# First mixer: decays by exp and tanh, its products on VectorE, the logarithm's series behind the pools

## The chip, the cores and the metric

The kernel runs on one core of a Trainium2 chip, as one launch. The metric is its time on the device in microseconds; below it is the median of three runs. A profile is one further execution, recorded by the hardware. The engines are named as in the profile: PE is TensorE's products, PEld its weight loads, DVE is VectorE, ACT is ScalarE, POOL is GpSimd, SP is the engine whose queue issues nearly all DMAs.

## The reference, cut to what matters

The program is a two-layer block, then a block with a recurrent part, a neighbourhood attention and 32 experts. The change lies in the first layer's mixer and in the keys of the cross attention behind it:

```python
def rg_lru(x, w_gx, b_gx, w_ga, b_ga, lam):
    xh = x.reshape(Bn, S, H_A, HD_A)
    gate_x = jax.nn.sigmoid(jnp.einsum('bshi,hij->bshj', xh, w_gx).reshape(Bn, S, W) + b_gx)
    gate_a = jax.nn.sigmoid(jnp.einsum('bshi,hij->bshj', xh, w_ga).reshape(Bn, S, W) + b_ga)
    log_a = -C_RG * gate_a * jax.nn.softplus(-lam)      # C_RG = 8
    a = jnp.exp(log_a)
    mult = jnp.sqrt(-jnp.expm1(2.0 * log_a))
    bx = mult * (gate_x * x)
    h = scan over time: h = a * h + bx
    return h

def mixer_ab(x, ...):                                   # x is 512 x 1024, float32
    z = rms_norm(x, norm) @ w_in                        # 1024 x (1024 gate, 1024 rec, 512 pool)
    xr = causal_dwconv(z_rec, conv_w, conv_b)           # 4 taps
    y_a = jax.nn.gelu(z_gate) * rg_lru(xr, w_gx, b_gx, w_ga, b_ga, lam)
    y_b = multi_scale_pool(z_pool, w_pool, b_pool, pool_scale)   # windows 2, 4, 8, 16
    return jnp.concatenate([y_a, y_b], axis=-1) @ w_out

def cross_attn(x, mem, ...):
    m = rms_norm(mem, mem_norm)                         # mem is 256 x 1024
    k = m @ wk;  v = m @ wv
```

The softplus of lam is a logarithm, which the kernel computes on 8 numbers per partition by a series.

## The kernel before, in words

Activations lie with the features on the 128 partitions and the 512 tokens along the row, so the eight tiles of a 1024 wide vector are called 0 to 7. Every product is made of three single ones (`mm3`, lines 522 to 524): weight and activation are each split into a rounded high part and the rest (whi and wlo, xn or act or tmp likewise), and high by high, high by low and low by high are added in PSUM.

Weights come as a stream of 1 MB chunks in the order of use. A chunk (tile raw, two buffers) is four pieces of 512 columns, a piece four blocks of 128 by 128, twelve products of one tile. For each piece ScalarE makes whi by a cast (line 352) and VectorE wlo by a subtraction (line 354). There are eight buffers of either, so a cast waits until TensorE has used the piece eight earlier, and a chunk is asked for (line 342, on SP) when the last wlo of the chunk two earlier is made. Pieces are numbered from 0 here; piece 36 is the first that the step O below uses, piece 32 the first of the chunk ahead of it.

The mixer runs along a string of steps:

`r0 m t0 m m r1 G m g0 t1 g1 r2 O s0 g2 r3 t2 s1 m g3 m s2 r4 r5 m t3 t4 s3 g4 g5 s4 m r6 t5 s5 r7 t6 g6 g7 t7 s6 s7`

Step r (`rec`, line 909) makes a tile of z_rec, its four taps and its split y; g (`gates`, line 918) two small products of y into aux tiles of PSUM and from them the decay al and the input; t (`gate`, line 937) the GELU branch; s (`scan`, line 943) the recurrence, its product with the GELU branch and the split act that the output product reads; G the group products of the pools and O their share of the output product; m a part of the memory's keys and values (`memory`, line 733). Ahead of the string stand the norm, the series of the logarithm (line 870 on), the head of `memory` with the spread of its rsqrt (lines 756 to 758), and the pools (line 951 on). A scheduler orders each engine's instructions by estimated times and priorities; an engine then runs them strictly in that order. So an instruction that waits holds up all that stand behind it on its engine, weight casts and wlo among them.

ScalarE's functions need tables: a change between the tables of tanh with exp, sqrt and gelu shows as an ACT_TABLE_LOAD of the line that needs it.

Of the kernel before, what the change touches and what calls it, by code (L numbers as in the profile page):

```python
# [8 lines left out]
F32 = mybir.dt.float32  # L9
F32R = mybir.dt.float32r  # L10
I32 = mybir.dt.int32
AF = mybir.ActivationFunctionType
ALU = mybir.AluOpType
# [3 lines left out]
P = 128  # L17
S = 512
D = 1024
DT = D // P  # L20
MEM = 256
# [72 lines left out]
def plan():  # L94
# [33 lines left out]
    for step in MIX.split():  # L128
# [12 lines left out]
        elif step[0] == "O":  # L141
            blocks("ab_w_out", 0, range(8, 12), range(8))
    memory(0, n)
    blocks("ab_w_out", 0, range(8), range(8), AHEAD)
    attn(0)
    ffn(0)
    for m in (0, 8, 4, 12):
        blocks("c_w_pw1", 0, range(8), range(m, m + 4), 4)
    memory(1)
    blocks("c_w_pw2", 0, range(8), range(8), AHEAD)  # L150
    attn(1)
# [291 lines left out]
class Kernel:  # L443
# [284 lines left out]
    def memory(self, l, act, kv):  # L728

        nc = self.nc  # L730
        raw = self.W.tile([P, DT, MEM], F32, name="raw", bufs=2)
        nc.sync.dma_start(raw, self.a["mem"])
        yield
        parts = []
        for i in range(4):
            h = act.tile([P, 2, MEM], F32R, name="act")
            lo = act.tile([P, 2, MEM], F32R, name="act")
            for j in range(2):
                g = self.v("xa_mem_norm", 8 * l + 2 * i + j)
                nc.scalar.activation(h[:, j], raw[:, 2 * i + j], AF.Copy, scale=g)  # L740
                nc.vector.scalar_tensor_tensor(lo[:, j], raw[:, 2 * i + j], g, h[:, j].bitcast(F32),
                                               op0=ALU.mult, op1=ALU.subtract)
                parts.append((h[:, j], lo[:, j]))
        acc = None
        for i in range(4):
            q = self.tmp()
            nc.scalar.activation(q, raw[:, 2 * i:2 * i + 2].rearrange("p a b -> p (a b)"), AF.Square)
            if acc is None:
                acc = q
            else:  # L750
                n = self.tmp()
                nc.gpsimd.tensor_add(n, acc, q)
                acc = n
        n = self.tmp()
        nc.gpsimd.tensor_add(n[:, :MEM], acc[:, :MEM], acc[:, MEM:])
        r = self.rsqrt(self.by_token(n, n=2), 2, 1.0 / D)
        rb = self.tmp()[:, :MEM]
        nc.vector.tensor_copy(rb, self.spread(r, 2))
        kh, kl = (kv.tile([P, DT, MEM], F32R, name="kv") for _ in range(2))
        vh, vl = (kv.tile([P, 2, D], F32R, name="kv") for _ in range(2))  # L760
        self.mem[l] = kh, kl, vh, vl
        yield
        for m in range(0, 8, 2):
            ps = self.acc()
            for j in range(2):
                for k in range(8):
                    self.mm3(ps[:, j * MEM:(j + 1) * MEM], self.st.block("xa_wk", l, k, m + j),
                             parts[k], k == 0, k == 7)
            t = self.tmp()
            nc.vector.tensor_mul(t.rearrange("p (a b) -> p a b", a=2),  # L770
                                 ps.rearrange("p (a b) -> p a b", a=2),
                                 rb[:, None, :].to_broadcast([P, 2, MEM]))
            h, lo = (z[:, m:m + 2].rearrange("p a b -> p (a b)") for z in (kh, kl))
            nc.scalar.copy(h, t)
            nc.vector.tensor_sub(lo, t, h.bitcast(F32))
            yield
        for c in range(4):
            w = [self.st.two("xa_wv", l, k, 2 * c) for k in range(8)]
            ps = self.acc()
            f = slice(c * MEM, (c + 1) * MEM)  # L780
            for t in range(2):
                ts = slice(t * P, (t + 1) * P)
                for k in range(8):
                    self.mm3(ps[:, t * MEM:(t + 1) * MEM], (parts[k][0][:, ts], parts[k][1][:, ts]),
                             w[k], k == 0, k == 7)
            z = self.tmp()
            for t in range(2):
                o = slice(t * MEM, (t + 1) * MEM)
                nc.scalar.activation(z[:, o], ps[:, o], AF.Copy, scale=r[:, t:t + 1])
            z = z.rearrange("p (a b) -> p a b", a=2)  # L790
            nc.scalar.copy(vh[:, :, f], z)
            nc.vector.tensor_sub(vl[:, :, f], z, vh[:, :, f].bitcast(F32))
            yield
# [70 lines left out]
    def mixer(self, act, kv):  # L864
        nc = self.nc
        T = self.tmp
        xs, rb = self.norm("ab_norm", 0, "ab_w_in", range(16, 20))


        lam = self.v("a_lambda", 0, 8)  # L870
        sm = lambda: self.M.tile([P, 8], F32, name="sp")
        ab, e, s, s2, pl = sm(), sm(), sm(), sm(), sm()
        nc.scalar.activation(ab, lam, AF.Abs)
        nc.scalar.activation(e, ab, AF.Exp, scale=-1.0)
        d = sm()
        nc.vector.tensor_scalar(d, e, 2.0, None, op0=ALU.add)
        rd = sm()
        nc.vector.reciprocal(rd, d)
        nc.vector.tensor_mul(s, e, rd)
        nc.vector.tensor_mul(s2, s, s)  # L880
        nc.vector.tensor_scalar(pl, s2, 1.0 / 17, 1.0 / 15, op0=ALU.mult, op1=ALU.add)
        for n in (13, 11, 9, 7, 5, 3, 1):
            p2 = sm()
            nc.vector.tensor_mul(p2, pl, s2)
            pl = sm()
            nc.vector.tensor_scalar(pl, p2, 1.0 / n, None, op0=ALU.add)
        lp = sm()
        nc.vector.tensor_mul(lp, pl, s)
        ng = sm()
        nc.vector.tensor_scalar(ng, lam, -1.0, 0.0, op0=ALU.mult, op1=ALU.max)  # L890
        sp = sm()
        nc.vector.scalar_tensor_tensor(sp, lp, 2.0, ng, op0=ALU.mult, op1=ALU.add)
        cc = self.C.tile([P, 8], F32, name="cc")
        nc.vector.tensor_scalar(cc, sp, -2.0, None, op0=ALU.mult)

        hb = self.C.tile([P, 16], F32, name="hb")
        nc.vector.tensor_scalar(hb, self.v("a_gate_x_b", 0, 16), 0.5, None, op0=ALU.mult)
        bs = self.C.tile([P, 4], F32, name="bs")
# [7 lines left out]
        xr, ge, ab = {}, {}, {}  # L906
# [11 lines left out]
        def gates(i):  # L918
            y, parts = xr.pop(i)
            px = self.dense([parts], "a_gate_x_w", i, range(1), 0, self.aux())  # L920
            pa = self.dense([parts], "a_gate_a_w", i, range(1), 0, self.aux())
            tx, t = T(), T()
            nc.scalar.activation(tx, px, AF.Tanh, bias=hb[:, i:i + 1], scale=0.5)
            nc.scalar.activation(t, pa, AF.Tanh, bias=hb[:, 8 + i:9 + i], scale=0.5)

            c = cc[:, i:i + 1]
            nc.scalar.activation(t, t, AF.Tanh, bias=c, scale=c)
            d, al = T(), T()
            nc.vector.tensor_scalar(d, t, -1.0, 1.0, op0=ALU.mult, op1=ALU.add)
            nc.vector.reciprocal(d, d)  # L930
            nc.vector.scalar_tensor_tensor(al, t, 1.0, d, op0=ALU.add, op1=ALU.mult)
            nc.scalar.activation(t, t, AF.Sqrt, scale=-1.0)
            nc.gpsimd.tensor_mul(t, t, d)
            nc.vector.scalar_tensor_tensor(tx, tx, 1.0, y, op0=ALU.add, op1=ALU.mult)
            nc.gpsimd.tensor_mul(tx, tx, t)
            ab[i] = al, tx

        def gate(i):
# [4 lines left out]
        def scan(i):  # L943
            al, bx = ab.pop(i)
            h = T()
            nc.vector.tensor_tensor_scan(h, al, bx, 0.0, op0=ALU.mult, op1=ALU.add)
            nc.gpsimd.tensor_mul(h, h, ge.pop(i))
            ya.append(self.split(h, act, "act"))


# [1 line left out]
        for g, w in enumerate((2, 4, 8, 16)):  # L952
            u = self.conv_in(self.dense(xs, "ab_w_in", 0, range(8), 16 + g), rb, 16)
            a, span = u, 1
            while span < w:
                b = T(16)
                nc.vector.memset(b[:, :16], 0.0)
                nc.vector.tensor_add(b[:, 16:], a[:, 16:], a[:, 16 - span:16 - span + S])
                a, span = b, 2 * span
            m = T()  # L960
            nc.vector.scalar_tensor_tensor(m, a[:, 16:], 1.0 / w, u[:, 16:], op0=ALU.mult,
                                           op1=ALU.subtract)
            f = self.M.tile([P, 16], F32, name="f")
            nc.vector.tensor_mul(f, a[:, 16:32], self.c("pool")[:, 16 * g:16 * g + 16])
            nc.vector.tensor_sub(m[:, :16], f, u[:, 16:32])
            pooled.append(self.split(m, act, "act"))
        yb = []

        def groups():
# [1248 lines left out]
```

## Time and profile before

| | |
|---|---|
| median of 3 runs | 2449.68 us (2449.46 to 2450.52) |
| the profiled execution | 2453.04 us |
| its span, first to last instruction | 2451.3 us, mean granted clock 0.979 |
| TensorE products busy | 2359.5 us, 96% |
| VectorE busy | 1403.8 us, 57% |
| ScalarE busy | 938.1 us, 38% |
| GpSimd busy | 359.6 us, 15% |

The busy shares are means over the whole span; the mixer is its first 250 us, where VectorE is much busier than that. The granted clock tells at which of its two levels, 1.2 or 2.4 GHz, TensorE ran. In a list of waits a row names the engine and tile that waited, and the one whose end released it. In a timeline a row is one run of instructions of one kind; what stands in brackets is the idle time just before it and what ended it.

### The profile page before, as it was taken

How to read it: one execution, taken by the hardware profiler on the slowest of the kernel's cores; microseconds unless marked ns; L12 is line 12 of the kernel's file. 1: busy time of each engine (PE TensorE's matmuls, PEld its weight loads, DVE VectorE, ACT ScalarE, POOL GpSimd, SP SyncE). 2: the span in 40 equal slices, each digit the busy share in tenths (PEclk: the TensorE clock that was granted, in tenths of full speed). 3: DMA queues.
4: the chain of work that ended last, by engine and by line, in shares of the span. 5: the costliest groups of instructions: out<-in, count | busy, mean ns of one | idle time of the engine just before them, and what ended most of it. 6: DMA issues, size and time to landing. Idle time of an engine off the chain costs nothing. (4 is left out here: it accounts for less than half of the span.)

```text
span 2451.3 us, 34809 instructions
## 1 busy us (share of the span) xinstructions
PE 2359.5 (96%) x13357; PEld 1830.2 (75%) x13357; DVE 1403.8 (57%) x2706; ACT 938.1 (38%) x1706; POOL 359.6 (15%) x361
## 2 busy tenths in 40 slices
PE   7999999999999999999999999999999989999996
PEld 6887888888888779788888888877876666764441
DVE  7988656545455455664645455688566766531110
ACT  4666444334244235543424234465233413321110
POOL 2112102101011000101101011211002221402211
PEclk9999999999999999999999999999889999989999
DMA  4332212222223213212222232466654435479998
GB/s 179 122 131 91 88 56 102 101 89 103 91 98 111 79 68 121 87 69 95 87 102 103 86 103 86 150 157 184 181 159 133 127 99 162 138 276 353 380 380 291
DMA packets 131196, 344.53 MB, mean 141 GB/s; under 512 B 40435, under 2 KB 66834, under 8 KB 101328
## 3 DMA queue, kind: packets, MB, share of 16 engines
q1 hardware_dynamic: 122944, 327.29, 38.7%
q0 software_dynamic: 5632, 10.49, 2.4%
q10 hardware_dynamic: 2448, 4.46, 0.5%
q8 instruction: 107, 1.75, 0.3%
q14 instruction: 65, 0.53, 0.1%
HBM read 307.33 MB, written 34.87 MB: 140 GB/s over the span
## 5 line engine op out<-in xcount | busy, mean ns | idle before, releaser
L352 ACT CAST whi<-raw 128x512 fp32r<-128x512 f32 x652 | 398.4, 620 | 710.3 <-PE acc L523 602.6
L522 PE MATMUL acc<-xn,whi 128*128 128x512 f32 x1656 | 656.6, 397 | 12.6 <-ACT xn L560 7.1
L354 DVE TENSOR_TENSOR wlo<-raw,whi 128x512 fp32r<-128x512 f32 x652 | 479.9, 742 | 307.3 <-ACT whi L352 304.3
L524 PE MATMUL acc<-xn,wlo 128*128 128x512 f32 x1656 | 651.5, 394 | 2.6 <-DVE wlo L354 2.6
L523 PE MATMUL acc<-xn,whi 128*128 128x512 f32 x1656 | 650.6, 393 | 0.0
L522 PEld LDWEIGHTS acc<-xn,whi 128*128 128x128 f32 x1656 | 312.9, 189 | 82.0 <-ACT xn L560 7.1
L524 PEld LDWEIGHTS acc<-xn,wlo 128*128 128x128 f32 x1656 | 312.6, 189 | 73.0 <-issue 3.8
L523 PEld LDWEIGHTS acc<-xn,whi 128*128 128x128 f32 x1656 | 313.1, 189 | 65.8 <-issue 1.6
L522 PE MATMUL acc<-act,whi 128*128 128x512 f32 (+1 forms) x676 | 251.3, 373 | 3.0 <-DVE tmp L1814 1.7
L523 PE MATMUL acc<-act,whi 128*128 128x512 f32 (+1 forms) x676 | 251.2, 372 | 2.7 <-DVE act L558 2.7
L524 PE MATMUL acc<-act,wlo 128*128 128x512 f32 (+1 forms) x676 | 251.0, 371 | 0.0
L721 POOL TENSOR_TENSOR tmp<-tmp 128x512 f32<-128x512 f32 x48 | 74.3, 1547 | 622.9 <-DVE tmp L719 555.8
L522 PEld LDWEIGHTS acc<-act,whi 128*128 128x128 f32 x676 | 128.3, 190 | 25.6 <-DVE tmp L1814 2.2
L523 PEld LDWEIGHTS acc<-act,whi 128*128 128x128 f32 x676 | 128.7, 190 | 25.0 <-DVE act L558 3.1
L524 PEld LDWEIGHTS acc<-act,wlo 128*128 128x128 f32 x676 | 128.5, 190 | 22.2
L580 POOL TENSOR_TENSOR tmp<-tmp 128x512 f32<-128x512 f32 x56 | 80.5, 1437 | 425.6 <-ACT tmp L573 405.1
L558 DVE TENSOR_TENSOR act<-tmp,act 128x512 fp32r<-128x512 f32 x88 | 61.1, 695 | 86.6 <-ACT act L557 84.6
L557 ACT CAST act<-tmp 128x512 fp32r<-128x512 f32 x88 | 54.4, 620 | 122.4 <-POOL tmp L721 91.2
L2096 POOL DMA_INDIRECT out<-tmp,tid x32 | 50.7, 1583 | 246.7 <-ACT tmp L2095 156.8
L701 DVE SCALAR_TENSOR_TENSOR tmp<-tmp,vec 128x512 f32<-128x512 f32 x96 | 72.2, 752 | 17.0 <-ACT tmp L698 15.3
L2064 PE MATMUL acc<-raw,xn 128*64 128x512 f32 x320 | 75.8, 602 | 4.5 <-DMA raw<-wex 4.5
L684 DVE TENSOR_TENSOR x<-x,acc 128x512 f32<-128x512 f32 x80 | 52.2, 681 | 39.5 <-PE acc L524 39.5
(438 smaller groups left out, 3176.8 us busy)
## 6 DMA issues: line engine op xcount, KB each, us to landing
raw<-wst SPq DMA_DIRECT2D x162, 1024.0 KB
raw<-wex SPq DMA_DIRECT2D x56, 1024.0 KB
whi<-wex SPq DMA_DIRECT2D x56, 256.0 KB
wlo<-wex SPq DMA_DIRECT2D x56, 256.0 KB
x<-wex SPq DMA_DIRECT2D x12, 1024.0 KB
bkv<-bkv SPq DMA_DIRECT2D x32, 192.0 KB
rec<-ab SPq DMA_DIRECT2D x8, 512.0 KB
sp_gate<-tmp ACTq DMA_DIRECT2D x16, 256.0 KB
```

The source lines that it names most:

```text
L352: self.nc.scalar.copy(hi, raw)
L354: self.nc.vector.tensor_sub(lo, raw, hi.bitcast(F32))
L522: nc.tensor.matmul(ps, w[0], x[0], start=first, stop=False)
L523: nc.tensor.matmul(ps, w[0], x[1], start=False, stop=False)
L524: nc.tensor.matmul(ps, w[1], x[0], start=False, stop=last)
L557: nc.scalar.copy(h, src)
L558: nc.vector.tensor_sub(lo, src, h.bitcast(F32))
L580: nc.gpsimd.tensor_add(n, accs.pop(), t)
L684: self.nc.vector.tensor_add(self.x[m], self.x[m], ps)
L701: nc.vector.scalar_tensor_tensor(z, h[:, k:k + S], taps[k], y, op0=ALU.mult, op1=ALU.add)
L721: nc.gpsimd.tensor_mul(z, u, ge)
L2064: nc.tensor.matmul(pg[a], h[:, o:o + SLOTS], w[2 * k + n], start=c + k == 0, stop=c + k == 4)
```

## The change

It has four parts. The memory's rsqrt is spread over the partitions (`spread`, line 598, and the copy into rb) only behind the first two tiles' products with xa_wk, and rb comes from another pool. The series of the logarithm is written behind the pools, tied there behind the last subtraction of the last pool; its last factor is -4 in place of -2. In `gates` the decay al is an Exp, and the factor of the input comes of a Tanh of the same argument, a Square and a Sqrt, so that the reciprocal and two of the VectorE operations go; the two products of POOL there and the one of `scan` become one of `gates` (with an addition) and two plain ones on VectorE.

```diff
@@ memory @@
         r = self.rsqrt(self.by_token(n, n=2), 2, 1.0 / D)
-        rb = self.tmp()[:, :MEM]
-        nc.vector.tensor_copy(rb, self.spread(r, 2))
...
                     self.mm3(ps[:, j * MEM:(j + 1) * MEM], self.st.block("xa_wk", l, k, m + j),
                              parts[k], k == 0, k == 7)
+            if m == 0:
+                rb = self.M.tile([P, S], F32, name="rb", bufs=2)[:, :MEM]
+                nc.vector.tensor_copy(rb, self.spread(r, 2))
@@ mixer: the series goes from ahead of the memory to behind the pools @@
-        lam = self.v("a_lambda", 0, 8)
-        nc.scalar.activation(ab, lam, AF.Abs)
-        nc.scalar.activation(e, ab, AF.Exp, scale=-1.0)
...
-        nc.vector.tensor_scalar(cc, sp, -2.0, None, op0=ALU.mult)
@@ gates @@
             c = cc[:, i:i + 1]
+            al, d = T(), T()
+            nc.scalar.activation(al, t, AF.Exp, bias=c, scale=c)
             nc.scalar.activation(t, t, AF.Tanh, bias=c, scale=c)
-            d, al = T(), T()
-            nc.vector.tensor_scalar(d, t, -1.0, 1.0, op0=ALU.mult, op1=ALU.add)
-            nc.vector.reciprocal(d, d)
-            nc.vector.scalar_tensor_tensor(al, t, 1.0, d, op0=ALU.add, op1=ALU.mult)
-            nc.scalar.activation(t, t, AF.Sqrt, scale=-1.0)
-            nc.gpsimd.tensor_mul(t, t, d)
+            nc.scalar.activation(d, al, AF.Square)
+            nc.vector.scalar_tensor_tensor(t, d, 1.0, t, op0=ALU.add, op1=ALU.mult)
+            nc.scalar.activation(t, t, AF.Sqrt, scale=-0.25)
             nc.vector.scalar_tensor_tensor(tx, tx, 1.0, y, op0=ALU.add, op1=ALU.mult)
-            nc.gpsimd.tensor_mul(tx, tx, t)
+            nc.vector.tensor_mul(tx, tx, t)
@@ scan @@
-            nc.gpsimd.tensor_mul(h, h, ge.pop(i))
+            nc.vector.tensor_mul(h, h, ge.pop(i))
@@ pools @@
-            nc.vector.tensor_sub(m[:, :16], f, u[:, 16:32])
+            it = nc.vector.tensor_sub(m[:, :16], f, u[:, 16:32]).ins
             pooled.append(self.split(m, act, "act"))
+        with self.tc.issue_after(it):
+            lam = self.v("a_lambda", 0, 8)
...
+            nc.vector.tensor_scalar(cc, sp, -4.0, None, op0=ALU.mult)
```

What the scheduler makes of it stands in the order of the instructions. First VectorE at the front of the program, behind the split of the input, before:

```order
L876 TENSOR_SCALAR sp<-sp 128x8
L878 RECIPROCAL sp<-sp 128x8
L879 TENSOR_TENSOR sp<-sp 128x8
...
L888 TENSOR_TENSOR sp<-sp 128x8
L890 TENSOR_SCALAR sp<-vec 128x8
L892 SCALAR_TENSOR_TENSOR sp<-sp 128x8
L354 TENSOR_TENSOR wlo<-raw,whi 128x512 x4
L894 TENSOR_SCALAR cc<-sp 128x8
L354 TENSOR_TENSOR wlo<-raw,whi 128x512 x4
L606 TENSOR_SCALAR rs<-aux 128x4
```

and now:

```order
L354 TENSOR_TENSOR wlo<-raw,whi 128x512
L561 SCALAR_TENSOR_TENSOR xn<-x_106,vec,xn 128x512 x2
L354 TENSOR_TENSOR wlo<-raw,whi 128x512 x8
L606 TENSOR_SCALAR rs<-aux 128x4
L613 TENSOR_SCALAR rs<-rs 128x4
```

The sp rows are the series; the wlo x4 and x4 are pieces 4 to 11. Nothing stands ahead of them now but the split xn.

Second VectorE at the memory's rsqrt (the rs rows of 128x2), before:

```order
L606 TENSOR_SCALAR rs<-aux 128x2
L354 TENSOR_TENSOR wlo<-raw,whi 128x512
L613 TENSOR_SCALAR rs<-rs 128x2
L614 TENSOR_SCALAR rs<-rs 128x2
L618 TENSOR_TENSOR rs<-rs 128x2
L619 SCALAR_TENSOR_TENSOR rs<-rs 128x2
L620 SCALAR_TENSOR_TENSOR rs<-rs 128x2
```

and now, where lines 930 to 934 are the pools:

```order
L606 TENSOR_SCALAR rs<-aux 128x2
L689 MEMSET tmp 128x16
L690 TENSOR_TENSOR tmp<-acc,rb 128x512
L613 TENSOR_SCALAR rs<-rs 128x2
L930 MEMSET tmp 128x16
L931 TENSOR_TENSOR tmp<-tmp 128x512
L614 TENSOR_SCALAR rs<-rs 128x2
L354 TENSOR_TENSOR wlo<-raw,whi 128x512
L618 TENSOR_TENSOR rs<-rs 128x2
L934 SCALAR_TENSOR_TENSOR tmp<-tmp 128x512
L619 SCALAR_TENSOR_TENSOR rs<-rs 128x2
```

The steps of the rsqrt now have the work of the pools between them. The series stands further on, mixed with pieces 20 to 29 in the same way.

Third ScalarE at the gates 0 and 1, before, from the Tanh of g0 (lines 923, 924) on; line 927 is the second Tanh, 932 the Sqrt, 941 the GELU:

```order
L923 ACTIVATE tmp<-aux,hb 128x512
L924 ACTIVATE tmp<-aux,hb 128x512
L352 CAST whi<-raw 128x512
L927 ACTIVATE tmp<-tmp,cc 128x512
L352 CAST whi<-raw 128x512 x6
L923 ACTIVATE tmp<-aux,hb 128x512
L932 ACT_TABLE_LOAD
L932 ACTIVATE tmp<-tmp 128x512
L941 ACT_TABLE_LOAD
L941 ACTIVATE tmp<-tmp 128x512
L924 ACTIVATE tmp<-aux,hb 128x512
```

and now, behind the Exp of g0 (line 902, with a table load of its own) and a cast; line 903 is the Tanh, 904 the Square, 906 the Sqrt, 897 and 898 the first two Tanh of g1, 914 the GELU:

```order
L903 ACTIVATE tmp<-tmp,cc 128x512
L904 ACTIVATE tmp<-tmp 128x512
L897 ACTIVATE tmp<-aux,hb 128x512
L914 ACT_TABLE_LOAD
L914 ACTIVATE tmp<-tmp 128x512
L906 ACT_TABLE_LOAD
L906 ACTIVATE tmp<-tmp 128x512
L898 ACT_TABLE_LOAD
L898 ACTIVATE tmp<-aux,hb 128x512
L352 CAST whi<-raw 128x512
```

Before, the first cast of this stretch is that of piece 36, the six behind it those of 37 to 42. Now pieces 34 and 35 are cast there, and the last row is that of piece 36. In the whole program there are five table loads more than before (26 and 31). SP's order is the same. On TensorE the spread of the memory's rsqrt stands behind 48 products of xa_wk; its other products keep their order but for the small ones of the gates.

## Rows read from the trace of the kernel before

**Rows 1.** Windows: length; busy PE, PEld, DVE, ACT, POOL; PE clock; DMA share; GB/s.
```profile
60.00:80.00 20.00, 20.00 (x135) 18.53 (x134) 19.79 (x44) 10.73 (x18) 0.00 (x0) 1.00 0.34 111
...
200.00:220.00 20.00, 16.73 (x72) 12.94 (x70) 20.00 (x27) 11.19 (x17) 5.95 (x4) 1.00 0.31 106
```

**Rows 2.** TensorE's waits from 0 to 450 us: total, times, longest.
```profile
PE aux L522 <- ACT tmp L557: 5.2, 3, 2.3
PE aux L590 <- POOL tmp L580: 2.9, 1, 2.9
PE acc L523 <- DVE act L558: 2.7, 1, 2.7
PE acc L524 <- DVE wlo L354: 2.6, 1, 2.6
PE aux L598 <- DVE rs L620: 1.4, 1, 1.4
PE acc L522 <- DVE tmp L957: 1.3, 1, 1.3
PE aux L523 <- DVE tmp L558: 1.0, 2, 0.7
```

**Rows 3.** Busy time in two stretches with a lowered clock, columns as in rows 1.
```profile
24.40:31.10 6.70, 4.08 (x10) 2.81 (x9) 6.32 (x22) 0.01 (x1) 0.00 (x0) 0.51 0.14 22
...
246.20:249.60 3.40, 2.82 (x7) 2.24 (x8) 3.26 (x4) 1.14 (x2) 1.57 (x1) 0.53 0.01 2
```

**Rows 4.** Timeline of TensorE: start, duration, instruction, idle before.
```profile
100.89 0.39 PE L522 MATMUL acc<-act,whi 128*128 128x512 f32 x1
...
142.66 0.49 PE L522 MATMUL aux<-tmp,whi 128*128 128x512 f32 x1 [1.79 <-ACT tmp L557]
```

**Rows 5.** Timeline of VectorE.
```profile
20.54 1.22 DVE L876 TENSOR_SCALAR sp<-sp 128x8 f32<-128x8 f32 x1
...
26.79 2.49 DVE L354 TENSOR_TENSOR wlo<-raw,whi 128x512 fp32r<-128x512 f32 x4
...
52.13 0.17 DVE L964 TENSOR_TENSOR f<-tmp,cst 128x16 f32<-128x16 f32 x1
52.24 0.67 DVE L690 TENSOR_TENSOR tmp<-acc,rb 128x512 f32<-128x512 f32 x1
...
77.44 1.29 DVE L354 TENSOR_TENSOR wlo<-raw,whi 128x512 fp32r<-128x512 f32 x2
```

**Rows 6.** Timeline of ScalarE.
```profile
83.46 2.18 ACT L352 CAST whi<-raw 128x512 fp32r<-128x512 f32 x4 [1.97 <-DMA raw<-wst]
...
89.72 0.78 ACT L973 ACTIVATE tmp<-acc,bs,vec 128x512 f32<-128x512 f32 x1
...
93.09 0.63 ACT L352 CAST whi<-raw 128x512 fp32r<-128x512 f32 x1
93.60 0.83 ACT L927 ACTIVATE tmp<-tmp,cc 128x512 f32<-128x512 f32 x1
...
98.68 0.68 ACT L923 ACTIVATE tmp<-aux,hb 128x512 f32<-128x512 f32 x1
99.49 1.28 ACT L932 ACT_TABLE_LOAD   x1
...
103.27 0.67 ACT L924 ACTIVATE tmp<-aux,hb 128x512 f32<-128x512 f32 x1
...
220.69 0.68 ACT L923 ACTIVATE tmp<-aux,hb 128x512 f32<-128x512 f32 x1
...
247.90 0.62 ACT L557 CAST act<-tmp 128x512 fp32r<-128x512 f32 x1 [4.77 <-POOL tmp L947]
```

**Rows 7.** Groups of equal instructions, VectorE and POOL, 40 to 290 us: busy, mean ns.
```profile
L354 DVE TENSOR_TENSOR wlo<-raw,whi 128x512 fp32r<-128x512 f32 x103 | 85.5, 848 | 13.6 <-ACT whi L352 13.6
L930 DVE RECIPROCAL tmp<-tmp 128x512 f32<-128x512 f32 x8 | 26.8, 3353 | 0.3
...
L933 POOL TENSOR_TENSOR tmp<-tmp 128x512 f32<-128x512 f32 x8 | 12.2, 1527 | 101.7 <-ACT tmp L932 101.7
```

## What the change will do to the time, predicted before it was run

> **What bounds the kernel now.** I read the engines' busy time in windows of 20 us first, then TensorE's waits, then the granted clock around them, then single rows of VectorE and ScalarE. TensorE is the engine that sets the end: in the windows it is busy 20.00 of 20 us wherever nothing makes it wait [rows 1]. All that the change touches ends before 250 us, and from there on the order of TensorE's work is the old one, so the change is worth what TensorE reaches that point earlier. Between 20 and 260 us VectorE is the neighbour to watch: 19.79 of 20 us busy at 60:80 and 20.00 at 200:220, where TensorE falls to 16.73 [rows 1]. TensorE's waits name the places [rows 2]: 2.6 for wlo (piece 4), 2.9 for POOL's sum of squares, 1.4 and 1.3 around the memory's rsqrt, 5.2 in three waits and 1.0 in two for the split y of the gates, 2.7 for the last scan's act. Each long wait is followed by a stretch at the 1.2 GHz level: 6.7 us at 0.51 around the first, 3.4 us at 0.53 at the last [rows 3].
>
> **The change part by part.** The sum is made on TensorE's arrival at four places, minus meaning earlier.
>
> *Front.* 23 small operations leave VectorE: they stand from 20.54 to 26.79, 6.25 us, ahead of wlo 4 to 7 [rows 5]. Now the wlo follow the last xn, so the wait of 2.6 goes. POOL's 2.9 ahead of it stays, since its cause isn't touched, and with it a slow stretch. Before, 2.6 of the 6.7 slow us were the wait itself; if the stretch is now 3.4 long, the 20 products up to the next sum of squares lose a little less than before: **-3.2**. If it is 6.7 long and filled with work, half of the extra 3.3 is lost, about -1; that is the poor end.
>
> *Memory.* The spread of the memory's rsqrt moves behind 48 products, and VectorE mixes the rsqrt's tiny steps with the pools' work instead of running them in a row. The waits 1.4 and 1.3 [rows 2] become, by my count of the VectorE rows now ahead of it, about 0.6 at the moved spread: **-2.1**. The ends are -2.7 (no wait) and 0 (the rsqrt as late as it was relative to TensorE). The products that used rb from a tmp tile now read it from another pool: nothing.
>
> *The series, again.* It runs now among pieces 20 to 28, where VectorE is 19.79 of 20 us busy. Dependent small operations with other work between them cost 0.11 each (52.13 to 52.24) [rows 5], so 23 cost 2.5 us. VectorE had gained more than that ahead of it, so its weight pieces should keep most of their distance to TensorE: **+0.3**, at most +2.5. Its two ScalarE operations stay early and cost nothing new. TensorE is then at -5.0 when it comes to O, which began at 100.89 [rows 4]: it would begin at 95.9.
>
> *A new wait at O.* O's first weights are piece 36. Before, its cast stood at 93.09, ahead of g0's third activation and of all table loads [rows 6]. In the new order it stands behind the whole chain of g0, the Tanh of g1 and four table loads. ScalarE can't begin this row of work before the raw chunk of piece 32 lands. That chunk is asked for when wlo 27 is done (the first of the two at 77.44) and landed at 83.46 [rows 5, 6], 5.3 later. wlo 27 now stands behind the kv splits, which wait for ScalarE's gelu; I take it 2 us earlier than before (bounds: 0 and 5), so ScalarE starts at 81.4. Up to piece 36 stand 11 casts at 0.53 (a 0.63 cast at 93.09, the next start at 93.60), 4 scalings of the pools at 0.67, 4 Tanh out of PSUM at 0.58, an Exp and a Tanh at 0.72 (0.78, 0.68 and 0.83 less 0.11 of overlap), Square, gelu and Sqrt at 0.53, and 4 loads. For a load I take 1.48: from 98.68 to 103.27 there are 4.59 us, less 0.58 and two 0.53 [rows 6], for two loads. Sum 5.8 + 2.7 + 2.3 + 1.4 + 1.6 + 5.9 = 19.8, so O begins at about 101.2, after an idle time of some 5.3 us. **All that the front gave is gone, +0.3 against before**, and a slow stretch follows: **+1.7** (3.4 us at half rate) to +3.4 (6.7 us, as at 24.4 [rows 3]). With the bounds on wlo 27 the beginning is 98.2 to 103.2.
>
> *Gates and scans.* RECIPROCAL, 3.35 us each, its TENSOR_SCALAR and the product for al leave VectorE, one product of 0.6 takes the place of two on POOL of 1.5, and a second replaces the scan's; eight times [rows 7]. VectorE's wlo took 848 ns on the mean at 40:290 against 0.64 in an undisturbed pair of 1.29 [rows 5, 7]; the long ones lie beside POOL's products, which are gone. So y3, y4 to y7 and the scans come earlier by 4 us or more per gate. TensorE's waits on y, 5.2 and 1.0 with some smaller ones [rows 2]: at g3 1.8 [rows 4] and the lower half's 0.3, with the restart and a slow stretch like that at 246.2 [rows 3] **-4.0**; at g4 and g5 **-0.6**; at g6 **-1.9**; at g7 2.3, of which 0.9 stays since ScalarE and VectorE are still queued there, **-1.5**. Last the scan of 7: from g6's first Tanh at 220.69 to the end of its act cast at 247.90 + 0.62 were 27.8 us, with both reciprocals and three POOL products in line [rows 6]. Now ScalarE's own row is 4 x 0.58 + 4 x 0.72 + 6 x 0.53 + 5 loads x 1.48 + 3 casts x 0.53 = 17.4, then product, scan, wlo, product and cast 3.5: 20.9, 7 us shorter, more than the wait of 2.7 [rows 2]. With the restart that is **-3.2**, and the stretch at 246.2 [rows 3] **-1.5**.
>
> *Sum.* 0.3 + 1.7 - 4.0 - 0.6 - 1.9 - 1.5 - 3.2 - 1.5 = -10.7, or -9.0 with the long slow stretch at O; I take -9.7. The profiled execution was 2453.04, so 2443.3 in its like; the median of the runs lies 3.4 below that execution: **2440.0**. From 250 us on TensorE's products are unchanged and carry it through, give or take 2 us for the slow stretches there.
>
> *A page against a row.* The rows give 1.48 us for a change of table, all told. The Trainium skill, page "ScalarE: Activation LUTs", section "What ACT_TABLE_LOAD costs", puts a change of set at about 2.66 us, the load of 1.28 (the trace agrees: 1.28 [rows 6]) and a drain that the rows here don't show. By it the four loads ahead of O would cost 4.7 more, by estimate, and the sum would be near -5.
>
> **Rivals.** *(a) Loads cost more in the new order.* A load that waits for the activation ahead of it or finds VectorE not ready stretches ScalarE's row; at 2.7 each (the two loads with their activations' whole length between 98.68 and 103.27 bound it from above, 4.59 less 0.58 less 1.28) O begins at 106, and the five loads of the last chain use up 6 of its 7 us: -10.7 + 4.9 + 1.7 + 2 = about -2, **2448**. For it: five more loads in all. Against it: the rows. *(b) ScalarE isn't late at O.* If wlo 27 keeps VectorE's whole lead of 5 us, or the scheduler's order lets the casts run ahead, O begins at 96 to 98 and the slow stretch is short or absent: -13 to -16, **2435**. *(c) Slower.* ScalarE's queue becomes the bound at each pair of gates: at g4/g5 the cast of piece 78 stands behind two Exp, two loads of sqrt and exp, four Tanh and a Square, some 10 us where before four casts followed one another. By TensorE's use the piece has about 6 us to spare. It decides from where a Sqrt waits more than 6 us for VectorE's product ahead of it, because VectorE has again 19 of 20 us of work; then pairs g0/g1, g4/g5 and g6/g7 each hold TensorE by 5 or more, with a slow stretch of 1.7 at each: -10.7 + 3 x 6.7 is +9, with only two of them +3 to +5, **2455**. *(d) The series isn't moved in effect.* The order shows its VectorE part behind the pools, so this is out but for its ScalarE part; and O would hide it, as it hides the front's gain.
>
> **How the numbers follow.** Forecast (-5 to -12.5): 0.52. (a) 0.17, (b) 0.19, (c) 0.10, (d) 0.02. A measurement can tell about 0.2%, 4.9 us. Faster by more: the forecast's most, 0.50, with (b) and (d) 0.71 and 0.04 of (a): 0.75. Within: the rest of the forecast and most of (a), 0.15. Slower: 0.10. The range leaves out the half of (b) below 2433 and (c): 2433 to 2449.
>
> **What would show it.** In the new trace: no wait on wlo L354 near 25; POOL's 2.9 still there; a wait under 1 at the spread; TensorE idle some 5 us ahead of its first product acc<-act,whi, released by ScalarE's whi, and a slow stretch after it; no waits above 1 on the split y between 140 and 215, none on act at 245; wlo mean near 0.69 us at 40:290; 5 more table loads. If O begins before 98, (b) is right; if after 104, (a). If whi waits stand at g4/g5, (c). If the waits at y remain at their old sizes, contention and reciprocals weren't what made y late, and the last four terms fall.

## The result, and the profile after

The changed kernel is faster: its time is 0.9929 of the kernel before, with a 95% interval from 0.991 to 0.9947, which on 2449.68 us is 13 to 22 us less, about 17. Its median over six runs was 2437.69 us (2430.95 to 2440.21), against 2453.86 (2449.46 to 2464.5) over six runs of the kernel before. In a second series on one chip, told below, the ratio was 0.9917 (0.9903 to 0.993). The forecast was 2440.0, faster, in a range of 2433 to 2449. The median lies only 2.3 us from it because the forecast started from the first three runs of the kernel before, 2449.68: as a difference, 9.7 us were forecast and about 17 measured.

The profiled execution took 2436.37 us with a span of 2434.6. TensorE's waits up to 450 us, in the columns of [rows 2]:

```profile
PE acc L522 <- ACT xn L560: 6.8, 1, 6.8
PE acc L522 <- ACT whi L352: 4.1, 1, 4.1
PE aux L590 <- POOL tmp L580: 1.6, 1, 1.6
PE aux L522 <- ACT tmp L557: 1.2, 1, 1.2
PE aux L598 <- DVE f L937: 0.7, 1, 0.7
PE acc L523 <- DVE tmp L558: 0.4, 1, 0.4
```

Against [rows 2], the 2.6 for wlo, the 2.7 for act and nearly all of the 5.2 and 1.0 for the split y are gone; 1.4 and 1.3 around the memory's spread became 0.7. One wait is new, 4.1 for whi. The timeline of TensorE shows its place, the first product of O, which stood at 100.89 before [rows 4]:

```profile
95.00 0.39 PE L524 MATMUL acc<-xn,wlo 128*128 128x512 f32 x1
99.50 0.79 PE L522 MATMUL acc<-act,whi 128*128 128x512 f32 x1 [4.11 <-ACT whi L352]
```

ScalarE ahead of it (timeline; line numbers are those of the changed kernel, 897 and 898 the first Tanh of a gate, 902 Exp, 903 Tanh, 904 Square, 906 Sqrt, 914 GELU):

```profile
79.99 0.62 ACT L352 CAST whi<-raw 128x512 fp32r<-128x512 f32 x1 [3.30 <-DMA raw<-wst]
...
88.62 1.28 ACT L902 ACT_TABLE_LOAD   x1
89.91 0.81 ACT L902 ACTIVATE tmp<-tmp,cc 128x512 f32<-128x512 f32 x1
...
93.07 1.28 ACT L914 ACT_TABLE_LOAD   x1
94.36 0.64 ACT L914 ACTIVATE tmp<-tmp 128x512 f32<-128x512 f32 x1
95.02 1.28 ACT L906 ACT_TABLE_LOAD   x1
96.31 0.63 ACT L906 ACTIVATE tmp<-tmp 128x512 f32<-128x512 f32 x1
96.95 1.28 ACT L898 ACT_TABLE_LOAD   x1
98.25 0.69 ACT L898 ACTIVATE tmp<-aux,hb 128x512 f32<-128x512 f32 x1
98.83 0.61 ACT L352 CAST whi<-raw 128x512 fp32r<-128x512 f32 x1
```

The row begins when the chunk of piece 32 has landed (79.99) and goes on to the cast of piece 36, which starts at 98.83, 18.8 us later: no gap worth naming, and four table loads in it. TensorE waits at O from 95.4 to 99.5 and then runs at half clock (windows; the columns as in [rows 1]):

```profile
94.40:99.50 5.10, 0.99 (x6) 0.49 (x4) 0.72 (x2) 5.04 (x7) 0.00 (x0) 0.89 0.32 137
99.50:105.20 5.70, 5.70 (x13) 4.41 (x14) 4.82 (x9) 5.67 (x9) 0.00 (x0) 0.50 0.01 3
```

VectorE between 40 and 290 us (groups, as in [rows 7]):

```profile
L354 DVE TENSOR_TENSOR wlo<-raw,whi 128x512 fp32r<-128x512 f32 x106 | 74.0, 712 | 30.8 <-ACT whi L352 30.6
```

The reciprocals' 26.8 us are gone, and a wlo takes 712 ns on the mean where it took 848.

To follow the gain along the program I compare when TensorE starts its n-th product, counted from 0, of the two traces (the order of the products differs only locally). Starts in us, worked out from the trace's rows:

```
product      before   changed   difference   what lies just ahead
   62         30.26     27.02       -3.2      the wait for wlo
  100         39.00     35.25       -3.7      the slow stretch behind it
  150         51.21     44.40       -6.8      the memory's spread (moved behind this product)
  204         58.99     53.07       -5.9      the spread where it stands now
  455        100.66     95.00       -5.7      last before O
  470        104.06    105.44       +1.4      O has begun
  680        148.64    145.90       -2.7      g3
  900        187.53    184.16       -3.4      g4, g5
 1060        227.64    220.72       -6.9      g6, g7
 1200        263.73    252.45      -11.3      the last act; the mixer's end
10000       1917.24   1905.88      -11.4
12000       2165.05   2148.94      -16.1
13356       2436.68   2420.55      -16.1      the last product
```

So 11.3 us come from the mixer, and in this pair of traces 4.8 more from behind 1917 us, where both kernels run the same instructions.

### The profile page after: what moved, and what is told of

It reads as the page before. It is cut to its first block, busy times and chain, and to the rows that moved or that the text cites. A ratio compares the mean times of both kernels' runs of the same rounds, so it can differ in the third digit from the quotient of the medians.

```text
span 2434.6 us, 34788 instructions
## 1 busy us (share of the span) xinstructions
PE 2356.5 (97%) x13357; PEld 1829.2 (75%) x13357; DVE 1365.2 (56%) x2706; ACT 954.1 (39%) x1727; POOL 322.6 (13%) x337
## 5 line engine op out<-in xcount | busy, mean ns | idle before, releaser
L354 DVE TENSOR_TENSOR wlo<-raw,whi 128x512 fp32r<-128x512 f32 x652 | 468.6, 724 | 321.2 <-ACT whi L352 318.0
L524 PEld LDWEIGHTS acc<-act,wlo 128*128 128x128 f32 x676 | 128.5, 190 | 22.6 <-DVE wlo L354 0.4
```

The lines of the kernel that those rows point to most:

```text
L354: self.nc.vector.tensor_sub(lo, raw, hi.bitcast(F32))
L524: nc.tensor.matmul(ps, w[1], x[0], start=False, stop=last)
```

## Experiments

All differences below are in the start of the 1200th product against the first trace of the kernel before (263.73), negative meaning earlier, since that is free of what happens later; the ratio with its interval is that of whole runs against the kernel before on the same chip.

**1. The series back at the front.** Theory: the front's gain is lost at O. Rival: it counts.

```diff
-        with self.tc.issue_after(it):      # behind the pools
-            lam = self.v("a_lambda", 0, 8)
...
+        lam = self.v("a_lambda", 0, 8)     # ahead of hb and the memory
...
+        nc.vector.tensor_scalar(cc, sp, -4.0, None, op0=ALU.mult)
```

> The changed kernel with the logarithm's series back at the front of VectorE; the memory's spread and the gates stay changed. Measured at TensorE's 1200th product, which the changed kernel reaches 11.3 us earlier than the kernel before. Theory (what the front gains is lost at O, since ScalarE's row of work sets when O begins): TensorE loses some 3 us at 25 to 30 (the wait for wlo of about 2.6 is back), comes to O later by that, but O begins within 1.5 us of the changed kernel's 99.5, and the product is reached 10 to 11.5 us earlier than before. Rival (each gain counts by itself): 3.2 us are lost for good, about 8 earlier.

Measured: the wait for wlo is back, TensorE comes to O 2.7 us later than in the changed kernel, and O begins at 100.70, 1.2 later, after a shorter wait:

```profile
100.70 0.50 PE L522 MATMUL acc<-act,whi 128*128 128x512 f32 x1 [2.62 <-ACT whi L352]
```

The slow stretch after it is shorter too, so the 470th product is 0.4 later and the 1200th **-11.26**, against -11.28. Moving the series brought nothing in this kernel by these traces. The ratio, 0.9952 (0.9927 to 0.9978), overlaps with that of the changed kernel.

**2. The gates alone.** The kernel before with the new `gates` and `scan` (and the factor -4); series and spread stay.

> The kernel before with the new gates and scan alone (Exp, Tanh, Square, Sqrt, products on VectorE); series and the memory's spread as before. Theory (ScalarE's row sets O): no gain up to 95 us, the raw chunk of piece 32 lands as before at 83.5, O begins some 20 us behind that, about 102.5 against 100.9, with a shorter wait than the 4.1 of the changed kernel; then the gains at y3, y6, y7 and the last act as in the changed kernel: the 1200th product 8 to 10 us earlier than before. Rival (the three parts add): 11.3 less the 5.7 that the front had gained at 95 us, 5.6 earlier.

Measured: **-9.7**, as the theory had it and not the -5.6 of a plain sum; ratio 0.9951 (0.9932 to 0.9971). One detail was wrong: TensorE was itself 3.2 us late at 95, so it came to O at 104 and found whi ready. It ran at a granted clock of 0.50 for 10.3 us from 22.6 and again for 6.8 from 49.9, where the waits around the memory's spread (2.0 and 1.3) lie; the first trace of the kernel before has 6.7 us at the first place and none at the second. The edit doesn't reach that place: the second trace of the kernel before (run 9) has the same stretch at 49.9.

**3. The front alone.** The changed kernel with the gates and the scan of before: series and spread moved, nothing else.

> The kernel before with the series and the memory's spread moved, and nothing else: gates with the reciprocal and POOL's products. Theory: 5.7 us earlier at 95 us and O begins at about 95.2 without a wait, since piece 36 is cast ahead of the table loads; later VectorE, which is as full as before, makes y3, y6 and y7 late, so that part of it is lost in longer waits there: the 1200th product 1 to 4 us earlier than before. Rival (the parts add, the front is worth what it has at 95): 5.7 earlier.

Measured: -5.5 at 95, O without a wait, then the longest wait for y of all, 3.1 us at g3, more at g4, g6 and g7 and 2.7 for act; **-3.2** at the 1200th product; ratio 0.9989 (0.9976 to 1.0003), no difference. The waits:

```profile
PE aux L522 <- ACT tmp L557: 4.7, 3, 3.1
PE acc L523 <- DVE act L558: 2.7, 1, 2.7
...
PE aux L522 <- ACT tmp L897: 1.4, 1, 1.4
```

**4. One step moved behind O.** If the wait at O is ScalarE's queue, it must go when g1 isn't ahead of O:

```diff
-MIX = "r0 m t0 m m r1 G m g0 t1 g1 r2 O s0 ...
+MIX = "r0 m t0 m m r1 G m g0 t1 r2 O g1 s0 ...
```

> The changed kernel with one step moved: g1 (the second gate) stands behind O in the string of steps. Theory (the wait ahead of O is ScalarE's queue: Tanh of g1 and three of four table loads ahead of the cast of piece 36): the wait of 4.1 and the slow stretch of 5 us behind it go, O begins at about 95.2, and what isn't lost again at the scans stays: the 1200th product 15 to 18 us earlier than before, against 11.3. Rival (VectorE and ScalarE are bound there as a whole, so that moving work only moves the wait): waits on y or act of the same sum appear at g2, s1 or g3, and the product stays 10 to 13 us earlier.

Measured: no wait at O, nothing lost behind it, **-18.1**. The wait at O and its slow stretch cost the changed kernel 6.8 us. The ratio is 0.9917 (0.9888 to 0.9946); by whole runs it can't be told from the changed kernel.

**5. The reciprocal and POOL, each by itself.** The changed kernel with its two products on POOL; then the changed kernel with the old decays, all products on VectorE:

```diff
-            nc.vector.tensor_mul(tx, tx, t)
+            nc.gpsimd.tensor_mul(tx, tx, t)
...
-            nc.vector.tensor_mul(h, h, ge.pop(i))
+            nc.gpsimd.tensor_mul(h, h, ge.pop(i))
```

> The changed kernel with its two plain products (the input's in the gates, the scan's) on POOL as before; reciprocal gone, tables as in the changed kernel. Tells what of the gain at y3, y6, y7 and the last scan is the reciprocal's and what the crowding by POOL. Theory (the reciprocal and its two companions, 4.6 us of VectorE per gate, are most of it; each product on POOL costs VectorE's neighbours 0.7 us and 0.9 more in its own chain): O as in the changed kernel, waits on y below 1.5, the last act about 2 us later, the 1200th product 9 to 11 us earlier than before. Rival (POOL's crowding is most of it): 4 to 7 earlier.

```diff
-            al, d = T(), T()
-            nc.scalar.activation(al, t, AF.Exp, bias=c, scale=c)
             nc.scalar.activation(t, t, AF.Tanh, bias=c, scale=c)
-            nc.scalar.activation(d, al, AF.Square)
-            nc.vector.scalar_tensor_tensor(t, d, 1.0, t, op0=ALU.add, op1=ALU.mult)
-            nc.scalar.activation(t, t, AF.Sqrt, scale=-0.25)
+            d, al = T(), T()
+            nc.vector.tensor_scalar(d, t, -1.0, 1.0, op0=ALU.mult, op1=ALU.add)
+            nc.vector.reciprocal(d, d)
+            nc.vector.scalar_tensor_tensor(al, t, 1.0, d, op0=ALU.add, op1=ALU.mult)
+            nc.scalar.activation(t, t, AF.Sqrt, scale=-1.0)
+            nc.vector.tensor_mul(t, t, d)
...
-            nc.vector.tensor_scalar(cc, sp, -4.0, None, op0=ALU.mult)
+            nc.vector.tensor_scalar(cc, sp, -2.0, None, op0=ALU.mult)
```

> The changed kernel with the old decays (Tanh, reciprocal, Sqrt, no further tables) but all their products on VectorE: POOL does nothing in the mixer. Theory (VectorE gets three products of 0.6 per gate and loses as much again of crowding, so that it stays full; the reciprocals stay in the chain): no wait at O, then waits on y as with the front alone, only the last act earlier by POOL's slower products: the 1200th product 3 to 6 us earlier than before (the front alone gave 3.2). Rival (POOL's crowding is what made y late): 8 or more earlier.

Measured: with POOL **-6.5**, ratio 0.9963 (0.9951 to 0.9976); with the reciprocal and without POOL **-19.0**, ratio 0.9896 (0.988 to 0.9911). My theory fell in both, the rivals' numbers came: without POOL's products y and act are in time though the reciprocals stay. What the reciprocals cost while POOL works too is not told by these runs: the first kernel has two products of POOL per gate where the kernel before has three, and comes to the gates later. In the second kernel there are five table loads fewer, no wait at O, and hardly a wait in the whole mixer:

```profile
PE acc L522 <- ACT xn L560: 7.0, 1, 7.0
PE aux L590 <- POOL tmp L580: 2.4, 1, 2.4
PE aux L590 <- POOL tmp L755: 0.6, 1, 0.6
PE acc L522 <- ACT whi L352: 0.5, 1, 0.5
PE acc L522 <- ACT act L557: 0.3, 1, 0.3
```

VectorE does keep its eight reciprocals there (groups, 40 to 290 us), and a wlo costs 716 ns, as little as in the changed kernel. Nor is VectorE less busy than before: 132.66 of the 140 us from 100 to 240, where the kernel before has 126.68.

```profile
L354 DVE TENSOR_TENSOR wlo<-raw,whi 128x512 fp32r<-128x512 f32 x107 | 75.6, 716 | 12.7 <-ACT whi L352 12.3 <-PE acc L523 0.3
L904 DVE RECIPROCAL tmp<-tmp 128x512 f32<-128x512 f32 x8 | 26.8, 3352 | 0.2
```

This kernel beats the one before, and its four runs (2430.23 to 2432.93) lie below the five of the changed kernel on the same chip (2434.75 to 2437.2), though the intervals of the two ratios overlap; its median of 2430.82 us is the lowest of the study.

**6. The products alone.** The kernel before with the three products of `gates` and `scan` on VectorE, and nothing else.

> The kernel before with one edit: the three products of gates and scan on VectorE in place of POOL. Decays with the reciprocal, series and spread as before. Theory, formed from the two runs with reciprocal and with POOL (POOL's products, by slowing VectorE beside them and by standing in the chains to y and act, are what made y and act late; the reciprocal could stay): front and O as before (0 at 95 and at O, give or take 1), the waits of 1.8 to 2.7 at g3, g6, g7 and the last act go, the 1200th product 10 to 13 us earlier than before. Rival (the lead of 7 us from the front was needed for y to be in time; with full VectorE the waits stay): 3 to 7 earlier.

Measured: **-9.2**, a little under the theory's 10 to 13; ratio 0.9954 (0.9938 to 0.9971). The front was 2.6 us late at 95, as it was 3.3 late in the second trace of the kernel before (run 9), so this isn't the edit's; from there on it gained 11.8, as much as the second kernel of run 5 (-7.2 at 95, -19.0 at the end). All waits on y and act above 0.5 are gone, without any lead from the front.

**7. POOL busy again, in no chain.** To part the crowding from the longer chains: the best kernel with three products per gate on POOL that nobody reads, at the places of the old ones.

```diff
             nc.vector.tensor_mul(t, t, d)
+            nc.gpsimd.tensor_mul(d, d, d)
...
             nc.vector.tensor_mul(tx, tx, t)
+            nc.gpsimd.tensor_mul(t, t, t)
...
-            nc.vector.tensor_mul(h, h, ge.pop(i))
+            q = ge.pop(i)
+            nc.vector.tensor_mul(h, h, q)
+            nc.gpsimd.tensor_mul(q, q, q)
```

> The kernel with the old decays and all products on VectorE (19.0 us earlier at the 1200th product, POOL idle) plus three products per gate on POOL whose results nobody reads, at the places of the old ones and in tiles already spent: POOL is as busy as in the kernel before, but stands in no chain. Theory (crowding: VectorE's instructions beside a POOL product take about twice their time): wlo's mean goes from 716 ns back to 800 or more at 40:290, VectorE is full again, and waits on y or act come back, 1200th product 6 to 13 us earlier than before. Rival (only the chains mattered, POOL's 1.5 against VectorE's 0.6): still 17 to 19 earlier.

Measured: **-3.4**, ratio 0.998 (0.9963 to 0.9996). The order of instructions on TensorE, VectorE and ScalarE is the same in both kernels, no wait on any of them is put down to the added products, and 15.6 us are lost: TensorE waits 4.3 for the split y, 2.3 for act and 1.9 for wlo, with slow stretches behind:

```profile
PE aux L522 <- ACT tmp L557: 4.3, 2, 2.3
PE acc L523 <- DVE act L558: 2.3, 1, 2.3
PE acc L523 <- DVE wlo L354: 1.9, 2, 1.6
```

VectorE's busy time can't tell the two kernels apart, 133.14 us between 100 and 240 against 132.66. The loss is larger than I expected, and it falls less on wlo (757 ns) than on what happens to stand beside POOL. The two products of `gates` are lines 907 and 909 in the best kernel, 907 and 910 in the one with POOL busy; first the best kernel, then the other:

```profile
L907 DVE TENSOR_TENSOR tmp<-tmp 128x512 f32<-128x512 f32 x8 | 5.5, 687 | 0.7 <-ACT tmp L906 0.7
L909 DVE TENSOR_TENSOR tmp<-tmp 128x512 f32<-128x512 f32 x8 | 5.5, 687 | 0.1
```

```profile
L354 DVE TENSOR_TENSOR wlo<-raw,whi 128x512 fp32r<-128x512 f32 x102 | 76.2, 757 | 11.1 <-ACT whi L352 10.7 <-PE acc L523 0.3
...
L910 DVE TENSOR_TENSOR tmp<-tmp 128x512 f32<-128x512 f32 x8 | 9.7, 1212 | 0.1
...
L907 DVE TENSOR_TENSOR tmp<-tmp 128x512 f32<-128x512 f32 x8 | 7.2, 896 | 0.8 <-ACT tmp L906 0.8
```

The 1212 is a mean of two kinds: all eight overlap a product of POOL, five took 1523 to 1531 ns and three 685 to 692. Where VectorE kept its 0.7 us it could be POOL that took longer: two of its products stretched to 2.63 (at 119.05) and 4.37 (at 139.86), with VectorE's rows of 677 to 679 ns inside them, where most took 1.33 to 1.55.

In the trace of the kernel before, between 40 and 260 us, 25 wlo overlapped a product of POOL and took 1310 ns on the mean, 66 did not and took 678. The Trainium skill, page "SBUF — State Buffer", section "Who interferes with whom", says that a VectorE instruction with two inputs in SBUF contends with a GpSimd instruction that reads SBUF; the wlo of this trace agree.

**8. Two table loads more.** The price of a load, on which a rival rested: a Sqrt of one column between g0's Exp and Tanh.

```diff
-            nc.scalar.activation(t, t, AF.Tanh, bias=c, scale=c)
+            if i == 0:
+                nc.scalar.activation(d[:, :1], al[:, :1], AF.Sqrt)
+                nc.scalar.activation(t, t, AF.Tanh, bias=c, scale=c)
+            else:
+                nc.scalar.activation(t, t, AF.Tanh, bias=c, scale=c)
```

> The changed kernel with a Sqrt of one column between g0's Exp and its Tanh, which brings two more table loads ahead of the cast of piece 36 (six in place of four) and a tiny operation; its result isn't used. Theory (a change of table costs its 1.28 us and little else, 1.4 by the rows of the changed kernel): O begins 2.9 us later than in the changed kernel, about 102.4. Rival (2.66 us for each change, as the Trainium skill has it on its page ScalarE: Activation LUTs, What ACT_TABLE_LOAD costs): 5.5 later, about 105.

Measured: O begins at 102.59, 3.1 us later than in the changed kernel.

```profile
91.42 1.28 ACT L904 ACT_TABLE_LOAD   x1
92.72 0.20 ACT L904 ACTIVATE tmp<-tmp 128x1 f32<-128x1 f32 x1
92.94 1.28 ACT L905 ACT_TABLE_LOAD   x1
94.23 0.82 ACT L905 ACTIVATE tmp<-tmp,cc 128x512 f32<-128x512 f32 x1
```

ScalarE's row began 0.2 later than in the changed kernel (80.16 against 79.99). The other 2.9 us hold two loads and a tiny activation (0.22 to the next start), so a load costs 1.4: its own 1.28, and the overlap that two activations in a row would have had. The 2.66 that the Trainium skill gives ("ScalarE: Activation LUTs", "What ACT_TABLE_LOAD costs") would have given 5.5, by estimate; here the measurement decides.

**9. The two kernels again.** What of the time lies behind the mixer?

> The changed kernel once more, to tell what of its 17 us is the change: by the traces the mixer gave 11.3, and 4.8 more came between 1990 and 2165 us, where both kernels run the same instructions. Theory (that part is not the change's: places of the second block where a short wait is or isn't followed by a stretch at half clock, and a transfer that lands late): the 1200th product is again 11.3 earlier than before, the rest of the span differs from the first trace by up to 5 us either way, and over five rounds the kernel is 9 to 14 us faster. Rival (the change helps the second block too): again 15 us or more.

> The kernel before once more, to see what its second block does in another execution. The changed kernel came out 6 to 8 us faster by the timed runs than its mixer explains. Theory (the first trace of before had bad luck there, near 1990 to 2165 us; nothing of the change reaches it): the 1200th product within 1 us of the first trace, and the rest of the span shorter by some 3 to 5 us. Rival (the second block is slower in the kernel before, whatever the execution): the same 4.8 us longer than in the changed kernel's trace.

Measured: the changed kernel again, 1200th product -12.4, rest of the span as in its first trace; ratio 0.9917 (0.9903 to 0.993). The trace is the theory's, the time the rival's, about 20 us. The kernel before again: 1200th product 1.7 later than in its first trace (3.3 later at 95), where the theory allowed 1, and the rest of the span 3.2 shorter, as it forecast. From the 1200th product to the last, in us, by trace:

```
before 2173.0, again 2169.8      changed 2168.1, again 2167.6
series at front 2172.9           gates alone 2171.7
front alone 2167.7               g1 behind O 2176.6
POOL products 2171.3             old decays, no POOL 2172.2
products alone 2179.9            idle POOL products 2166.1
two loads more 2168.0
```

TensorE's products there are the same in all of them, and they spread by 13.8 us. One place of it, by windows: the changed kernel, then the one with the series at the front.

```profile
1832.00:1840.00 8.00, 8.00 (x86) 5.17 (x88) 3.63 (x14) 1.56 (x7) 6.16 (x18) 0.98 0.19 58
```

```profile
1832.00:1840.00 8.00, 8.00 (x47) 4.80 (x48) 2.33 (x9) 0.52 (x2) 4.61 (x14) 0.50 0.21 67
```

TensorE is busy in both, at 0.98 and at 0.50 of its clock; between the 8000th and the 10000th product the second kernel lost 5.4 us. The spread goes largely with that clock: behind the mixer TensorE was granted the lower level for 68.3 us in the shortest of these traces (2166.1) and for 102.4 in the longest (2179.9), for 78.5 in both traces of the kernel before, and for 71.7 and 68.3 in those of the changed one.

Of the two traces each, 12.7 us of the difference between the two kernels lie in the mixer and 3.5 behind it. The timed runs show 17 and 20 us, and their mean granted clocks, which hold the mixer too, speak against the luck of two traces: 0.981 or 0.982 in the five runs of the changed kernel in the second series, 0.973 to 0.980 in the fifteen of the kernel before on the same chip. Why a change in the first 250 us shifts the slow stretches so much later stays open, and so does how much of the 17 and 20 us is owed to it.

## Why the prediction was right, step by step

*The front, -3.2 and -2.1.* Measured -3.7 behind the slow stretch and -2.2 across the memory's spread (-5.9 at the 204th product). The wait for POOL's sum of squares, held fixed in the working, was 1.6 in place of 2.9, but it is 1.7 in the second trace of the kernel before too. For the series I had 0.3: 0.3 are lost from there to O, but 0.5 in run 1, where the series stands at the front (-3.5 to -3.0), so no cost of the series shows. TensorE was at -5.7 ahead of O; I had -5.0.

*The new wait at O.* This was the step that the sum turned on, and it held: O at 99.50 (101.2 forecast), idle 4.1 (5.3), ScalarE's row 19.4 from the landing to the end of piece 36's cast (19.8). What moved O was mostly the chunk of piece 32, which landed 1.4 us earlier than I took it; a load was 1.42 where I had 1.48. The slow stretch was between my two lengths: 5.7 us (99.5 to 105.2). Net +1.4, forecast +2.0. Runs 1, 4 and 8 show that the queue is the cause, and that it hides what the front gains.

*Gates and scans.* The terms were -4.0, -0.6, -3.4 for g6 and g7 together, and -4.7 for the last act with its slow stretch. Measured -4.1, -0.6, -3.5 and -4.4, but that each term fits is luck in part: the second traces of the two kernels (run 9) give -2.5, -1.9, -3.7 and -3.2 at the same places. The sum holds in both, -12.7 and -11.4. Part of the difference is the clock's: not each long wait is followed by a slow stretch, as I had read it. None came behind the 2.3 at g7 in the first trace of the kernel before, nor behind the 1.8 at g3 and the 2.7 for act in its second, though a stretch at g3 and one at the last act were in the terms. One sign failed narrowly: a wait of 1.2 on y stayed at 210.

The sizes are right in sum and the cause that stood first is wrong. I wrote that y comes earlier since the reciprocal and its two companions leave VectorE and since POOL's products no longer crowd it, and costed the sum of both. Runs 5 to 7 part them: without POOL the waits go with the reciprocal still there, and with POOL's work they are back. The step that failed is the one that took 26.8 busy us for the weight and 848 against 0.64 for a side effect. With POOL out of the mixer the reciprocals cost about 1 us (the table below); the doubled short rows stand wherever POOL happens to run, in the chains to y and act among other places.

*The rivals.* (a), dearer loads, is out by run 8. (b), O without a wait, didn't come in the changed kernel; run 4 shows its -18 when g1 is out of the way. (c), ScalarE's queue holding TensorE at the later pairs, didn't come: no wait for whi stands behind O. (d) was rightly put aside, and that the front's gain doesn't matter is run 1.

*The sum.* The terms gave -10.7 and I took -9.7; the mixer gave -11.3 and, in a second pair of traces, -14.1 (-12.4, against a start of before that was 1.7 later). The "2 us either way" for what lies behind 250 us was too small: it spread by 13.8 between traces, and the few us by which the timed difference exceeds the mixer's are there.

*What the change is worth, part by part.* Behind O, from the 470th product to the 1200th, against the first trace of the kernel before (POOL as to the gates and scans):

```
new decays, POOL idle      changed -12.7, again -13.0, series at front -13.1,
                           gates alone -12.9, g1 behind O -12.8, two loads more -13.0
old decays, POOL idle      run 5 -11.8, products alone -11.8
new decays, POOL products  -8.1
old decays, POOL products  front alone +2.3
old decays, unread ones    +3.8
kernel before again        -1.6
```

Where POOL is idle the gain is the same whether TensorE comes to O 7.2 us early or some 3 late. So the products off POOL are worth 11.8 there, and the new decays about 1 more. At O the new decays cost 7.0 when TensorE comes there early, as in the changed kernel, and nothing when it comes late (run 2). Series and spread alone gave 5.5 at 95 us, which shrank to **-3.2** at the waits on y and act; in the changed kernel the wait at O takes all of it. The second kernel of run 5 keeps its lead of 7.2, has no wait at O and gains the 11.8: that is the -19.0. Some 1.6 of it is not the edit's: this trace has no slow stretch at the front, where the changed kernel's first has one, and the changed kernel's second trace, which has none either, is 0.8 earlier at 95 than its first.

## What to carry to other kernels

When two engines share a stage, ask what the one does to the rows of the other beside it before asking what its own work costs: here work that nobody read cost 15.6 us. Before trading VectorE's arithmetic for ScalarE's functions, write down ScalarE's row up to the next weight cast, table loads included; a queue that runs in order turns four loads into a wait of TensorE and a slow stretch behind it. And test a compound change one part at a time: this one holds a part that gains 11.8 us in the mixer, and one that gains about 1 more there and gives 7.0 back at O.

## What the runs showed of the hardware

I had not expected how much POOL costs its neighbour: a product of VectorE on 128 by 512 takes 687 ns alone, and of eight that overlapped a POOL product five took 1523 to 1531 (run 7). Nor had I expected that twenty-six busy microseconds of reciprocals on an engine that is 19 of 20 us busy cost TensorE about 1 us (runs 5 and 6). After an idle time of 4.1 TensorE ran at a granted clock of 0.50 for 5.7 us; after 2.6 (run 1) for 3.4; after 2.7 in the second trace of the kernel before (246.9 to 249.6) not at all, at 1.00. Tanh shares a table with both GELU and Exp, and these two don't share one: a Tanh right behind a GELU brought no load (102.73 and 103.27 in the kernel before), an Exp behind such a Tanh brought one (88.62 in the changed kernel), a Tanh behind that Exp none (91.14), and the GELU after it one (93.07). And in the second block the same instructions ran at 0.98 or at 0.50 of the clock in different kernels, which alone moves the time by 5 us.
